# Block sums from VectorE to GpSimd, more result buffers, and four row blocks by way of HBM, in a two-layer float32 decoder trunk

## The chip, the cores and the metric

The kernel runs on one core of a Trainium2 chip. The core has five engines that each take their instructions in order: PE (TensorE: matrix products and transposes, weights loaded beside them as PEld), DVE (VectorE), ACT (ScalarE), POOL (GpSimd) and SP (SyncE, which here only issues DMAs). They work beside each other and wait for each other by semaphores. The metric is the time of one execution on the device, in microseconds (us), lower is better.

## The reference, cut to what matters

A trunk of two layers over 1024 tokens of 1024 features, all in float32. Layer 0 mixes tokens by latent attention (MLA), layer 1 by a gated linear recurrence (HGRN2); each is followed by a squared-ReLU MLP with 4096 hidden features. Every part stands between two RMS norms and adds to the residual stream.

```
def sq_relu_mlp(h, w1, w2):
    a = jax.nn.relu(h @ w1)
    return (a * a) @ w2

for layer in range(DEPTH):
    a = rms_norm(h, norm_gains[layer, 0])
    m = mla_mixer(a, ...) if layer % 2 == 0 else hgrn2_mixer(a, ...)
    h = h + rms_norm(m, norm_gains[layer, 1])
    a = rms_norm(h, norm_gains[layer, 2])
    h = h + rms_norm(sq_relu_mlp(a, mlp_w1[layer], mlp_w2[layer]), norm_gains[layer, 3])
```

## The kernel before

A float32 product is made of three products of halves: `split` writes a rounded high part (ACT, L75) and the rest (DVE, L76), and `mm3` (L80 to L82) multiplies high by high, high by low and low by high. Most of ACT's and DVE's work is such splits of weights (tile `w`) that SP has loaded into a `raw` tile. There are two `raw` tiles beside each other and five `w` tiles in turn.

The stages in the trace are MLA with its output projection (to about 500 us), the first MLP's up-projection (to 840) and down-projection (to 1165), HGRN2 (to 1735), and the second MLP's up- (to 2110) and down-projection (to the end). Both MLP projections use a seven-product block scheme after Strassen: sums of blocks are formed first, seven products take the place of eight, and results are added up.

*Up-projection*, `mlp_up`. The activations lie transposed as four blocks (`A` and `whole`). `tsums` (L736 to L742 hold half of its eight sums for each of two k) makes four further blocks T1 to T4 from them, 128x1024 values each time. The weights come in 16 blocks p. For the first eight (EARLY) a first loop makes the products that need no T; ACT copies and squares these into `h` tiles (L771, L772; L780 for the copy), which go to HBM (`psp`, `hsp`). Then a second loop runs `others` for all p: four weight-block sums of 128x512 (L793, L794, L796, L797) into `s` tiles, their splits, five products, nine additions of results (L801 to L833), and seven results to HBM from POOL's queue (`spill`, L768). For early p, SP loads back the two results. The `h` tiles are a ring of 10 (layer 0) or 8 (layer 1), the `s` tiles of 3.

*Down-projection*, `mlp_down`. In two halves c, and in each the seven products i = 0, 1, 4, 2, 5, 6, 3 with four block pairs q: the left factor is loaded from `hsp` (`raw`, `sx`), the right is a weight block or a sum of two (t1 to t4, less22; L921, L930, L935, L939, L996; 128x1024). `gather` adds up results (L982). In the second half of the first MLP the rows are finished on the way (`finish_rows`: mean square on ACT, power on POOL, L196 and L197 on DVE, a store to `res` from SP, L198, and the norm for the next part, L201). `into_features` transposes such a row block on PE (L174) and splits it into `A`.

*HGRN2.* Sixteen steps (token half, head), with projections by `featproj` (sigmoid of f on ACT, L1094), an elementwise part and `core_products`. The first eight steps use the first four row blocks of `A` (tokens 0 to 511), the last eight the other four.

A scheduler decides the order of the instructions on each engine from the program's order and priorities; `LAG` holds offsets by which transposes are put later. SP's loads of one kind keep the program's order.

## Time and profile before

| | |
|---|---|
| three timed runs | 2417.41, 2423.98, 2420.9 us; median 2420.9 |
| profiled execution | 2420.12 us |
| its span, first to last instruction | 2418.4 us |
| granted TensorE clock, mean | 0.980 |
| instructions | 30758 |

The profile is a page with busy shares by engine and groups of instructions, and a trace that can be asked for each engine's waits, for windows and for a timeline. In a group's row stand line, engine, operation, output<-inputs, shape and count, then busy us, mean ns of one, and the engine's idle time just before such instructions with what ended it. In the timeline a row holds start, duration, engine, line and operation, and in brackets the idle time before it. PEclk is the granted clock of TensorE as a share of full speed. Where the time goes is shown with the prediction.

### The profile page before, as it was taken

To read this page: it belongs to the slowest core of one execution; us is meant where nothing else is said; L and a number is where in the kernel's file an instruction comes from. 1 tells how busy PE (TensorE), PEld (TensorE's weight loads), DVE (VectorE), ACT (ScalarE), POOL (GpSimd) and SP (SyncE) were. 2 spreads that over 40 slices of the span, in tenths; PEclk is the share of its full clock that TensorE was granted. 3 is DMA by queue.
4 is the path that set the end of the run, shared out by engine and by line. 5 is a ranking of instruction groups with operands and counts; after the bars stand their busy time and mean duration, and the time that the engine had idled before them with its cause. 6 is when DMAs were issued, how large, how long until landed. Compare 5 with 4: busy or idle time off the path is not lost. (4 is left out here: it accounts for less than half of the span.)

```text
span 2418.4 us, 30758 instructions
## 1 busy us (share of the span) xinstructions
PE 2292.8 (95%) x11487; PEld 1926.0 (80%) x11487; DVE 1615.8 (67%) x2311; ACT 1178.3 (49%) x1910; POOL 343.2 (14%) x686
## 2 busy tenths in 40 slices
PE   9999999978999999999899999999888999999988
PEld 8889998757788778877688888888666778888876
DVE  5658884575766566578765667756776766576578
ACT  5445554453444444434656556665453445443433
POOL 1300000111211200001232213321211212100002
PEclk9999999989999999999899999999999999999999
DMA  6100002565554574544612224222455544664644
GB/s 214 31 22 10 10 10 92 200 198 166 202 174 144 176 284 141 183 174 140 200 53 88 77 89 126 84 70 85 142 178 196 180 161 141 219 250 131 232 143 164
DMA packets 228388, 337.32 MB, mean 139 GB/s; under 512 B 16871, under 2 KB 136718, under 8 KB 228238
## 3 DMA queue, kind: packets, MB, share of 16 engines
q1 hardware_dynamic: 209038, 272.42, 34.8%
q0 software_dynamic: 19200, 62.93, 7.0%
q8 instruction: 90, 1.47, 0.3%
q14 instruction: 60, 0.49, 0.1%
HBM read 253.51 MB, written 81.79 MB: 139 GB/s over the span
## 5 line engine op out<-in xcount | busy, mean ns | idle before, releaser
L76 DVE TENSOR_TENSOR w<-raw,w 128x1024 fp32r<-128x1024 f32 (+1 forms) x256 | 279.0, 1094 | 193.8 <-ACT w L75 192.9
L75 ACT ACTIVATE w<-raw 128x1024 fp32r<-128x1024 f32 (+1 forms) x256 | 241.6, 948 | 228.5 <-PE mm L82 122.4
L80 PE MATMUL mm<-A,w 128*128 128x512 f32 x832 | 330.7, 398 | 15.5 <-ACT h L771 11.0
L75 ACT ACTIVATE w<-s 128x1024 fp32r<-128x1024 f32 x156 | 165.2, 1060 | 347.4 <-PE c L82 124.7
L81 PE MATMUL mm<-A,w 128*128 128x512 f32 x832 | 329.0, 395 | 1.0 <-DVE A L76 1.0
L82 PE MATMUL mm<-A,w 128*128 128x512 f32 x832 | 326.6, 393 | 0.0
L76 DVE TENSOR_TENSOR w<-s,w 128x1024 fp32r<-128x1024 f32 x156 | 190.5, 1222 | 113.3 <-ACT w L75 113.1
L143 POOL TENSOR_TENSOR rstd<-rstd,nhalf 128x1 f32<-128x1 f32 x56 | 61.8, 1105 | 1056.9 <-DVE rstd L142 963.2
L80 PEld LDWEIGHTS mm<-A,w 128*128 128x128 f32 x832 | 158.1, 190 | 55.6 <-ACT h L771 16.1
L768 POOL DMA_DIRECT2D hsp<-h x224 | 121.2, 542 | 479.0 <-ACT h L772 229.0
L82 PEld LDWEIGHTS mm<-A,w 128*128 128x128 f32 x832 | 158.4, 190 | 33.2
L81 PEld LDWEIGHTS mm<-A,w 128*128 128x128 f32 x832 | 158.4, 190 | 32.8 <-DVE A L76 1.4
L81 PE MATMUL mm<-w,w 128*128 128x512 f32 x432 | 171.3, 397 | 10.6 <-DVE w L76 10.5
L82 PE MATMUL mm<-w,w 128*128 128x512 f32 x432 | 169.7, 394 | 0.0
L80 PE MATMUL mm<-w,w 128*128 128x512 f32 x432 | 155.2, 394 | 12.4 <-ACT w L75 6.5
L80 PE MATMUL mm<-w,A 128*128 128x256 f32 (+2 forms) x384 | 120.7, 316 | 3.3 <-ACT A L75 3.1
L82 PE MATMUL mm<-w,A 128*128 128x256 f32 (+2 forms) x384 | 120.3, 315 | 0.0
L81 PE MATMUL mm<-w,A 128*128 128x256 f32 (+2 forms) x384 | 119.3, 312 | 0.0
L771 ACT ACTIVATE h<-h 128x512 f32<-128x512 f32 x96 | 60.0, 625 | 106.4 <-DVE h L812 69.8
L80 PEld LDWEIGHTS mm<-w,w 128*128 128x128 f32 x432 | 81.9, 190 | 32.3 <-ACT w L75 9.5
L81 PEld LDWEIGHTS mm<-w,w 128*128 128x128 f32 x432 | 82.2, 190 | 31.7 <-DVE w L76 14.8
L82 PE MATMUL c<-T,w 128*128 128x512 f32 x256 | 98.7, 389 | 1.2 <-DVE w L76 1.2
(394 smaller groups left out, 5671.3 us busy)
## 6 DMA issues: line engine op xcount, KB each, us to landing
hsp<-h POOLq DMA_DIRECT2D x224, 256.0 KB, 3.0
raw<-in_mlp_w_dram SPq DMA_DIRECT2D x108, 512.0 KB, 3.9
s<-in_mlp_w_dram SPq DMA_DIRECT2D x80, 512.0 KB, 7.2
raw<-hsp SPq DMA_DIRECT2D x76, 512.0 KB, 4.0
raw<-in_hgrn_w_in_dram SPq DMA_DIRECT2D x64, 512.0 KB, 4.1
sx<-hsp SPq DMA_DIRECT2D x36, 512.0 KB, 4.0
res<-xt SPq DMA_DIRECT2D x24, 512.0 KB, 3.7
xt<-res SPq DMA_DIRECT2D x22, 512.0 KB, 4.5
```

The lines of the kernel that those rows point to most:

```text
L75: ACT.activation(dst[:, 0], src, AF.Copy)
L76: DVE.tensor_tensor(dst[:, 1], src, dst[:, 0].bitcast(F32), ALU.subtract)
L80: PE.matmul(ps, lhs[0], rhs[0], start=start, stop=False, skip_group_check=more)
L81: PE.matmul(ps, lhs[0], rhs[1], start=False, stop=False, skip_group_check=more)
L82: PE.matmul(ps, lhs[1], rhs[0], start=False, stop=stop, skip_group_check=more)
L143: POOL.tensor_tensor(r, r, nhalf[:, :1], ALU.pow)
L768: POOL.dma_start(hsp[i, p * P:(p + 1) * P, :], h)
L771: ACT.activation(h, src, AF.Relu)
```

## The change

1. The four weight-block sums in `others` go from DVE to POOL, in both layers (128 instructions), as do four of the eight T sums for each k (a and e: 16 instructions) and the five kinds of block sum in `mlp_down` (80 instructions).
2. The tile `whole` gets a pool of its own that is closed after `tsums`; in its place come further result buffers `h2` (4 in layer 0, 8 in layer 1), used by every odd call of `h512`.
3. `finish_rows` issues its store from POOL's queue instead of SP's. Its input tile can be loaded ahead (`rows_in`, into `s11` tiles); the last down-projection uses the same.
4. At the end of the first MLP the row blocks 4 to 7 are no longer transposed: POOL stores them in HBM (`later`), and in steps 2 to 5 of HGRN2 SP loads one each into a raw tile, where it is transposed and split into `A`.
5. `LAG` loses an entry, and its third is 250 instead of 150.

```diff
@@ -35,7 +35,7 @@
 ROPE_BASE = 10000.0
-LAG = (150, 100, 150, 300)
+LAG = (150, 100, 250)
 EARLY = 8
@@ -88,6 +88,7 @@
     ysp = new(dram, [S, D // 2], F32, "ysp")
+    later = new(dram, [S // 2, D], F32, "later")
@@ -185,17 +186,18 @@
-    def finish_rows(wp, y, ms, gpost, gpre, src, dst, t, xt_bufs=2):
+    def finish_rows(wp, y, ms, gpost, gpre, src, dst, t, xt_bufs=2, xt=None):
         rows = slice(t * P, (t + 1) * P)
-        xt = new(wp, [P, D], F32, "xt", xt_bufs)
-        tc.keep_in_program_order(SP.dma_start(xt, src[rows, :]))
+        if xt is None:
+            xt = new(wp, [P, D], F32, "xt", xt_bufs)
+            tc.keep_in_program_order(SP.dma_start(xt, src[rows, :]))
         if ms is None:
...
         DVE.scalar_tensor_tensor(xt, y, r, xt, ALU.mult, ALU.add)
-        SP.dma_start(dst[rows, :], xt)
+        POOL.dma_start(dst[rows, :], xt)
         if gpre is not None:
@@ -650,7 +652,8 @@
-            A["whole"] = new(p, [P, 4, KT // 2, P], F32, "whole")
+            act["whole"] = ExitStack()
+            A["whole"] = new(pool(act["whole"], "whole", side="right"), [P, 4, KT // 2, P], F32, "whole")
@@ -733,13 +736,13 @@
                     split(T2[:, :, k:k + 2], d)
-                    DVE.tensor_tensor(by_tile(a), by_tile(part(B22, 0)), b12, ALU.subtract)
-                    DVE.tensor_tensor(a, a, part(B22, 1), ALU.add)
+                    POOL.tensor_tensor(by_tile(a), by_tile(part(B22, 0)), b12, ALU.subtract)
+                    POOL.tensor_tensor(a, a, part(B22, 1), ALU.add)
                     split(T1[:, :, k:k + 2], b)
...
                     e = d
-                    DVE.tensor_tensor(e, part(B21, 0), d, ALU.subtract)
-                    DVE.tensor_tensor(e, e, part(B21, 1), ALU.add)
+                    POOL.tensor_tensor(e, part(B21, 0), d, ALU.subtract)
+                    POOL.tensor_tensor(e, e, part(B21, 1), ALU.add)
                     split(T4[:, :, k:k + 2], e)
@@ -747,7 +750,12 @@
+            hs = {"n": 0, "more": None}
+
             def h512():
+                hs["n"] += 1
+                if hs["more"] and hs["n"] % 2:
+                    return new(hs["more"], [P, 512], F32, "h2", 4 if layer == 0 else 8)
                 return new(wp, [P, 512], F32, "h", 10 if layer == 0 else 8)
@@ -790,11 +798,11 @@
                 s34 = new(wp, [P, 1024], F32, "s", 3).rearrange("p (k c) -> p k c", c=256)
-                DVE.tensor_tensor(s12[:, :, :P], rA[:, :, P:], rB[:, :, P:], ALU.add)
-                DVE.tensor_tensor(s12[:, :, P:], s12[:, :, :P], rA[:, :, :P], ALU.subtract)
+                POOL.tensor_tensor(s12[:, :, :P], rA[:, :, P:], rB[:, :, P:], ALU.add)
+                POOL.tensor_tensor(s12[:, :, P:], s12[:, :, :P], rA[:, :, :P], ALU.subtract)
                 wS12 = w_parts(s12)
-                DVE.tensor_tensor(s34[:, :, :P], rA[:, :, :P], rA[:, :, P:], ALU.subtract)
-                DVE.tensor_tensor(s34[:, :, P:], rB[:, :, :P], s12[:, :, P:], ALU.subtract)
+                POOL.tensor_tensor(s34[:, :, :P], rA[:, :, :P], rA[:, :, P:], ALU.subtract)
+                POOL.tensor_tensor(s34[:, :, P:], rB[:, :, :P], s12[:, :, P:], ALU.subtract)
                 b = new(PG, [P, 512], F32, "tr")
@@ -840,6 +848,9 @@
             tsums()
+
+            act["whole"].close()
+            hs["more"] = pool(act["stack"], f"more{layer}", side="right")
             for p in range(NP):
@@ -918,7 +929,7 @@
                     load11(q)
-                    DVE.tensor_tensor(s11[q], b12, s11[q], ALU.subtract)
+                    POOL.tensor_tensor(s11[q], b12, s11[q], ALU.subtract)
                     return s11[q]
@@ -927,16 +938,16 @@
                     t = new(wr, [P, 2, 512], F32, "s12", 3)
-                    DVE.tensor_tensor(t, s22[q], s11[q], ALU.subtract)
+                    POOL.tensor_tensor(t, s22[q], s11[q], ALU.subtract)
                     return t
...
                     b12 = load12(q)
-                    DVE.tensor_tensor(b12, s22[q], b12, ALU.subtract)
+                    POOL.tensor_tensor(b12, s22[q], b12, ALU.subtract)
                     return b12
...
                 def t4(q):
-                    DVE.tensor_tensor(s21[q], s21[q], s11[q], ALU.add)
+                    POOL.tensor_tensor(s21[q], s21[q], s11[q], ALU.add)
                     return s21[q]
@@ -957,9 +968,11 @@
-                def by_tiles(i, banks, right, n1, done, own_tile):
+                def by_tiles(i, banks, right, n1, done, own_tile, then=None):
                     fs = [factors(i, q, right, own_tile) for q in qs[n1:]]
+                    if then is not None:
+                        then()
                     for tt in range(4):
@@ -993,7 +1006,7 @@
                 def less22(q):
-                    DVE.tensor_tensor(s21[q], s21[q], s22[q], ALU.subtract)
+                    POOL.tensor_tensor(s21[q], s21[q], s22[q], ALU.subtract)
@@ -1011,6 +1024,12 @@
                 gather(c22, Y, c22)
+                def rows_in(t):
+
+                    xt = new(wp, [P, 2, 512], F32, "s11", KC // 2).rearrange("p a b -> p (a b)")
+                    tc.keep_in_program_order(SP.dma_start(xt, src[t * P:(t + 1) * P, :]))
+                    return xt
+
                 if not last:
@@ -1024,17 +1043,14 @@
                         DVE.tensor_tensor(c21[t], Y[t], U[t], ALU.add)
-                        finish_rows(wp, y[4 + t], None, gpost, gpre, src, dst, 4 + t)
-                        with tc.high_priority(offset=-LAG[3]):
-                            into_features(y[4 + t], act["A"], 4 + t)
+                        finish_rows(wp, y[4 + t], None, gpost, gpre, src, dst, 4 + t, xt=xts[t])
+                        POOL.dma_start(later[t * P:(t + 1) * P, :], y[4 + t])
                     product(3, Y, t4, True, n1=2)
-                    by_tiles(3, Y, t4, 2, done, False)
+                    xts = []
+                    by_tiles(3, Y, t4, 2, done, False, lambda: xts.extend(rows_in(4 + t) for t in range(4)))
                 else:
-                    xts, s22s, yg = {}, {}, {}
-                    for t in range(4, NT):
-                        xts[t] = new(wp, [P, D], F32, "xf", 2) if t < 6 else new(wp, [P, D], F32, "xt", 2)
-                        SP.dma_start(xts[t], src[t * P:(t + 1) * P, :])
+                    s22s, xts = {}, []
                     for t in range(4):
@@ -1042,7 +1058,7 @@
                         rows = slice((4 + t) * P, (5 + t) * P)
-                        xt = xts[4 + t]
+                        xt = xts[t]
                         DVE.tensor_tensor(c21[t], Y[t], U[t], ALU.add)
@@ -1052,7 +1068,7 @@
-                    by_tiles(3, Y, t4, 0, done, True)
+                    by_tiles(3, Y, t4, 0, done, True, lambda: xts.extend(rows_in(4 + t) for t in range(4)))
                     sr.close()
@@ -1275,6 +1291,11 @@
                 proj_v(half, h // 2)
+            if 1 < si < 6:
+
+                r = raw_tile()
+                SP.dma_start(r, later[(si - 2) * P:(si - 1) * P, :])
+                into_features(r, A, si + 2)
             with tc.high_priority(offset=100):
@@ -1286,7 +1307,8 @@
                 gpre = row_bcast(wp, "gpre", norm_gains[1, 2], D)
-                acc = new(pool(act["stack"], "acc", side="right"), [P, 4, D], F32, "acc")
+                act["whole"] = ExitStack()
+                acc = new(pool(act["whole"], "acc", side="right"), [P, 4, D], F32, "acc")
```

Three places show how the instructions stand.

At the end of the first MLP, on PE: `mm` here are HGRN2's projections, `tr` the transposed rows y4 to y7. Before:

```order
L82 MATMUL mm_1607_10020<-w_1604_9966,A10_1511_9503 128x256
L174 MATMUL tr_1541_9678<-ident_5_64,y4_1227_7509 128x128 x4
L174 MATMUL tr_1542_9685<-ident_5_64,y4_1227_7509 128x128 x4
L174 MATMUL tr_1551_9725<-ident_5_64,y5_1228_7510 128x128 x4
L174 MATMUL tr_1552_9732<-ident_5_64,y5_1228_7510 128x128 x4
L174 MATMUL tr_1561_9772<-ident_5_64,y6_1229_7511 128x128 x4
L174 MATMUL tr_1562_9779<-ident_5_64,y6_1229_7511 128x128 x4
L174 MATMUL tr_1571_9819<-ident_5_64,y7_1230_7512 128x128 x4
L174 MATMUL tr_1572_9826<-ident_5_64,y7_1230_7512 128x128 x4
L80 MATMUL mm_1618_10120<-A00_1509_9501,w_1617_10117 128x512
```

At the same place after:

```order
L80 MATMUL mm_1600_9977<-w_1597_9923,A10_1512_9512 128x256
L81 MATMUL mm_1600_9977<-w_1597_9923,A10_1512_9512 128x256
L82 MATMUL mm_1600_9977<-w_1597_9923,A10_1512_9512 128x256
L80 MATMUL mm_1611_10077<-A00_1510_9510,w_1610_10074 128x512
L81 MATMUL mm_1611_10077<-A00_1510_9510,w_1610_10074 128x512
L82 MATMUL mm_1611_10077<-A00_1510_9510,w_1610_10074 128x512
```

The eight groups of four transposes are gone; the next projection (`mm`, with `A00`) follows the last one at once.

In the last half of the second layer's down-projection, on DVE (`s11`, `s12`, `s21`, `s22`: weight blocks and their sums; `w`: their splits). Before:

```order
L76 TENSOR_TENSOR w_2988_18748<-raw_2987_18746,w_2988_18748 128x1024
L76 TENSOR_TENSOR w_2991_18756<-s11_2990_18753,w_2991_18756 128x1024
L76 TENSOR_TENSOR w_2993_18785<-sx_2992_18783,w_2993_18785 128x1024
L996 TENSOR_TENSOR s21_2959_18533<-s21_2959_18533,s22_2999_18829 128x1024
L930 TENSOR_TENSOR s12_3019_18977<-s22_2999_18829,s11_2980_18679 128x1024
L939 TENSOR_TENSOR s21_2959_18533<-s21_2959_18533,s11_2980_18679 128x1024
L996 TENSOR_TENSOR s21_2963_18567<-s21_2963_18567,s22_3003_18864 128x1024
L930 TENSOR_TENSOR s12_3023_19011<-s22_3003_18864,s11_2985_18716 128x1024
L76 TENSOR_TENSOR w_2996_18793<-s11_2995_18790,w_2996_18793 128x1024
L76 TENSOR_TENSOR w_2998_18826<-raw_2997_18824,w_2998_18826 128x1024
```

After, DVE:

```order
L76 TENSOR_TENSOR w_2991_18744<-s11_2990_18741,w_2991_18744 128x1024
L76 TENSOR_TENSOR w_2993_18773<-raw_2992_18771,w_2993_18773 128x1024
L76 TENSOR_TENSOR w_2996_18781<-s11_2995_18778,w_2996_18781 128x1024
L76 TENSOR_TENSOR w_2998_18810<-sx_2997_18808,w_2998_18810 128x1024
L76 TENSOR_TENSOR w_3001_18818<-s11_3000_18815,w_3001_18818 128x1024
L76 TENSOR_TENSOR w_3003_18851<-raw_3002_18849,w_3003_18851 128x1024
L76 TENSOR_TENSOR w_3005_18856<-s22_3004_18854,w_3005_18856 128x1024
L76 TENSOR_TENSOR w_3007_18886<-raw_3006_18884,w_3007_18886 128x1024
```

And the sums of that place, now on POOL:

```order
L1009 TENSOR_TENSOR s21_2964_18558<-s21_2964_18558,s22_3004_18854 128x1024
L941 TENSOR_TENSOR s12_3024_19002<-s22_3004_18854,s11_2985_18704 128x1024
L1009 TENSOR_TENSOR s21_2968_18592<-s21_2968_18592,s22_3008_18889 128x1024
L941 TENSOR_TENSOR s12_3028_19036<-s22_3008_18889,s11_2990_18741 128x1024
L950 TENSOR_TENSOR s21_2964_18558<-s21_2964_18558,s11_2985_18704 128x1024
L1009 TENSOR_TENSOR s21_2972_18626<-s21_2972_18626,s22_3012_18924 128x1024
L941 TENSOR_TENSOR s12_3032_19070<-s22_3012_18924,s11_2995_18778 128x1024
L950 TENSOR_TENSOR s21_2968_18592<-s21_2968_18592,s11_2990_18741 128x1024
```

The splits stand one behind the other on DVE; the sums that stood between them are in POOL's order, among themselves.

In the first layer's `tsums`, on DVE (`s`: sums, `T1` to `T3`: their splits, `w`: a split of the early loop). Before:

```order
L731 TENSOR_TENSOR s_910_5408<-s_910_5408,A00_745_4340 128x1024
L733 TENSOR_TENSOR s_911_5409<-A11_747_4342,s_910_5408 128x1024
L736 TENSOR_TENSOR s_909_5407<-A11_747_4342,whole_748_4343 128x1024
L76 TENSOR_TENSOR T1_852_5070<-s_910_5408,T1_852_5070 128x1024
L734 TENSOR_TENSOR s_911_5409<-s_911_5409,A11_747_4342 128x1024
L737 TENSOR_TENSOR s_909_5407<-s_909_5407,A11_747_4342 128x1024
L730 TENSOR_TENSOR s_913_5427<-whole_748_4343,A00_745_4340 128x1024
L76 TENSOR_TENSOR w_879_5220<-raw_875_5199,w_879_5220 128x512
L76 TENSOR_TENSOR T2_849_5067<-s_911_5409,T2_849_5067 128x1024
L731 TENSOR_TENSOR s_913_5427<-s_913_5427,A00_745_4340 128x1024
L76 TENSOR_TENSOR T3_850_5068<-s_909_5407,T3_850_5068 128x1024
```

After, on POOL, whose stores of the early loop (`psp`, `hsp`) stand around the sums:

```order
L847 DMA psp_849_5067<-h_858_5095 128x512
L739 TENSOR_TENSOR s_910_5411<-A11_748_4343,whole_749_4347 128x1024
L740 TENSOR_TENSOR s_910_5411<-s_910_5411,A11_748_4343 128x1024
L847 DMA psp_849_5067<-h_865_5137 128x512
L776 DMA hsp_848_5066<-h_860_5113 128x512
L744 TENSOR_TENSOR s_912_5413<-A10_747_4342,s_912_5413 128x1024
L745 TENSOR_TENSOR s_912_5413<-s_912_5413,A10_747_4342 128x1024
```

And on ACT, where the split into `T3` reads POOL's sum `s_910`:

```order
L75 ACTIVATE T1_853_5074<-s_911_5412 128x1024
L779 ACTIVATE h_860_5113<-mm_857_5082 128x512
L788 ACTIVATE h_865_5137<-mm_864_5124 128x512
L75 ACTIVATE w_880_5224<-raw_876_5203 128x512
L75 ACTIVATE T2_850_5071<-s_912_5413 128x1024
L780 ACTIVATE h_860_5113<-h_860_5113 128x512
L75 ACTIVATE T3_851_5072<-s_910_5411 128x1024
L75 ACTIVATE T1_853_5074<-s_914_5431 128x1024
L75 ACTIVATE w_887_5266<-raw_883_5245 128x512
L779 ACTIVATE h_867_5155<-mm_864_5124 128x512
L788 ACTIVATE h_872_5179<-mm_871_5166 128x512
```

The two sums for T3 (L736 and L737 before) stand on POOL now, and ACT's T3 split still stands ahead of the next Relu and copy of early results (L779, L788).

## The prediction

> **What bounds the kernel now.** I read the page's busy shares first, then TensorE's waits, then windows around the widest waits, then the timeline of the engine each wait names.
>
> ```profile
> PE 2292.8 (95%) x11487; PEld 1926.0 (80%) x11487; DVE 1615.8 (67%) x2311; ACT 1178.3 (49%) x1910; POOL 343.2 (14%) x686
> ```
>
> TensorE (PE) is busy for 95% of the 2418.4 us span; VectorE (DVE) for 67%, GpSimd (POOL) for 14%. The matmuls are the same in number after the change, so all it can win is in the 5% in which PE stands still or runs at a lower clock. Taking time off DVE wins nothing by itself; it wins where PE waits for DVE. TensorE's waits, by what released them:
>
> ```profile
> PE mm L80 <- ACT h L771: 11.0, 12, 3.3
> PE tr L80 <- DVE h L801: 10.6, 2, 7.5
> PE mm L81 <- DVE w L76: 10.5, 8, 4.4
> PE tr L174 <- DVE acc L201: 9.5, 2, 5.1
> PE tr L174 <- DVE A L76: 8.9, 3, 4.2
> PE tr L82 <- DVE w L76: 6.0, 6, 1.6
> PE mm L80 <- DVE y L982: 5.9, 3, 3.8
> ```
>
> (The columns: who waits, for whom, total us, times, longest.) Five of these seven rows the change can reach: L771 and L801 (up-projection), w L76 on L81 and y L982 (down-projection), and A L76 (end of the first MLP). The acc row is the end of hgrn, where PE's order stays and the chain of products, norm and transposes is the same: nothing there. Of the tr L82 row I count nothing.
>
> **Why DVE is late.** Engines take instructions in order. DVE's own groups show what holds it:
>
> ```profile
> L793 DVE TENSOR_TENSOR s<-raw,raw 128x512 f32<-128x512 f32 x32 | 22.1, 691 | 47.0 <-DMA raw<-in_mlp_w_dram 47.0
> L935 DVE TENSOR_TENSOR s<-s,s 128x1024 f32<-128x1024 f32 x16 | 19.6, 1225 | 17.4 <-DMA s<-in_mlp_w_dram 17.3
> L921 DVE TENSOR_TENSOR s<-s,s 128x1024 f32<-128x1024 f32 x16 | 19.5, 1221 | 15.1 <-DMA s<-in_mlp_w_dram 15.1
> L996 DVE TENSOR_TENSOR s<-s,s 128x1024 f32<-128x1024 f32 x16 | 19.5, 1220 | 11.9 <-DMA s<-in_mlp_w_dram 11.9
> ```
>
> The last number is DVE's idle time in front of the group: 47.0 + 17.4 + 15.1 + 11.9 = 91 us in which a block sum at the head of DVE's queue waits for a load, and whatever stands behind it waits too. All four groups go to POOL. One such place, in the second layer's down-projection, DVE's timeline (start, duration), then PE's:
>
> ```profile
> 2302.60 1.23 DVE L996 TENSOR_TENSOR s<-s,s 128x1024 f32<-128x1024 f32 x1 [5.26 <-DMA s<-in_mlp_w_dram]
> 2303.74 1.22 DVE L930 TENSOR_TENSOR s<-s,s 128x1024 f32<-128x1024 f32 x1
> 2304.88 1.22 DVE L939 TENSOR_TENSOR s<-s,s 128x1024 f32<-128x1024 f32 x1
> 2306.01 1.22 DVE L996 TENSOR_TENSOR s<-s,s 128x1024 f32<-128x1024 f32 x1
> 2307.15 1.22 DVE L930 TENSOR_TENSOR s<-s,s 128x1024 f32<-128x1024 f32 x1
> 2308.28 1.22 DVE L76 TENSOR_TENSOR w<-s,w 128x1024 fp32r<-128x1024 f32 x1
> ...
> 2309.56 0.79 PE L81 MATMUL mm<-w,w 128*128 128x512 f32 x1 [4.38 <-DVE w L76]
> ```
>
> DVE sits 5.26 us on a load, does five sums (5.7 us), and only then the weight split that PE stood 4.38 us for. After the change the split has no sum before it.
>
> **The change, part by part.** The sum is made against the profiled execution, 2420.1 us (span 2418.4 and 1.7 us around it); the three timed runs have median 2420.9, so the two are taken as one.
>
> *Amount moved.* Off DVE: 128 sums of 128x512 at 0.69 us (88 us) and 96 of 128x1024 at 1.22 us (117 us): 205 us, 13% of its busy time. That is no gain yet. What they cost on POOL, by the rows nearest:
>
> ```profile
> L1145 POOL TENSOR_TENSOR e<-f 128x512 f32<-128x512 f32 x16 | 17.4, 1087 | 0.0
> L463 POOL TENSOR_TENSOR qrt<-ra,rb 128x256 f32<-128x256 f32 x8 | 6.0, 746 | 13.3 <-DVE rb L461 13.2
> L768 POOL DMA_DIRECT2D hsp<-h x224 | 121.2, 542 | 479.0 <-ACT h L772 229.0 <-DVE h L823 166.5 <-DVE h L826 34.1
> ```
>
> A 128x512 sum takes 1.09 us (L1145, same shape), at most 1.49 (twice L463); a 128x1024 sum, which no row shows, 2.2 us (twice L1145), at most 3.0. POOL gains 128 x 1.09 + 96 x 2.2 = 350 us on 343: far from full over the span.
>
> *Down-projection (80 sums).* Per pair of blocks PE works 24 matmuls; at the pace between these two starts, 0.23 us, that is 5.5 us.
>
> ```profile
> 2316.13 0.40 PE L82 MATMUL c<-w,w 128*128 128x512 f32 x1
> 2316.36 0.40 PE L80 MATMUL c<-w,w 128*128 128x512 f32 x1
> ```
>
> DVE keeps two splits (2.44 us), POOL has one sum (2.2 us); even one after the other, 4.7 us fit in 5.5. In passes with two sums per pair they need not (6.8), as two on DVE did (4.9); those sums are wanted a pass later, so they can spread. PE's waits here are 10.5 + 5.9 = 16.4 us, and behind each PE resumes at a lower clock: in the window from 2300 PEclk is 0.83, so 3.4 of 20 us, of which the waits themselves are part. I put the whole at 22 us and take half, **-11** (0 to -22): half, because a sum that waits for a late load is still waited for, on POOL, by the product that needs it.
>
> ```profile
> 1180.00:1200.00 20.00, 11.13 (x66) 9.74 (x66) 16.14 (x20) 10.24 (x19) 6.53 (x17) 0.73 0.77 234
> 1200.00:1220.00 20.00, 16.66 (x76) 13.37 (x75) 12.19 (x15) 15.96 (x21) 7.82 (x18) 0.76 0.09 33
> 2300.00:2320.00 20.00, 13.50 (x46) 10.28 (x45) 17.40 (x17) 6.57 (x7) 0.00 (x0) 0.83 0.36 124
> ```
>
> (Window; length; busy us and instructions of PE, weight load, DVE, ACT, POOL; PEclk; DMA share; GB/s.)
>
> *End of the first MLP.* PE has the transposes of y4 to y7 in its order, each behind ACT's and DVE's finishing of that row:
>
> ```profile
> 1189.59 1.97 PE L174 MATMUL tr<-ident,y 128*128 128x128 f32 x8 [3.21 <-DVE A L76]
> 1195.75 1.97 PE L174 MATMUL tr<-ident,y 128*128 128x128 f32 x8 [4.19 <-DVE A L76]
> 1199.19 1.97 PE L174 MATMUL tr<-ident,y 128*128 128x128 f32 x8 [1.48 <-DVE A L76]
> 1202.90 0.80 PE L80 MATMUL mm<-A,w 128*128 128x512 f32 x1 [1.74 <-ACT f L1094]
> ```
>
> The three waits are 8.9 us, at clocks 0.73 and 0.76. They go. What is late next is ACT's first sigmoid (L1094): ACT still takes the mean squares of y4 to y7 first, and PE's products of the first head wait for what follows. That chain also runs through DVE, where the 8 splits of A go from between the rows:
>
> ```profile
> L76 DVE TENSOR_TENSOR A<-tr,A 128x512 fp32r<-128x512 f32 x40 | 26.6, 684 | 3.3 <-ACT A L75 3.3
> ```
>
> It ends about 8 x 0.68 = 5.5 us sooner, and PE's head start beyond that is lost in waiting for the sigmoid. The transposes return in hgrn at full clock: four rows at 1.97 x 0.73 = 1.4 us, 5.8 us of PE as against 7.9 here. The four stores and four loads of `later` lie on POOL's and SP's queues, 512 KB each, two hgrn steps ahead of their use. I take **-6** (0 to -14, the waits and the clock's share).
>
> *Up-projection behind the T sums.* Reachable waits: 10.6 (L801) + 11.0 (L771) - 3.3 (the longest, inside the early phase) = 18 us. L793's 47 us at the head of DVE's queue go to POOL's, where the spills (0.54 us each, 7 per p) queue behind them instead; the extra `h2` buffers take up that delay. Half again: **-9** (0 to -18).
>
> *T sums (16 sums).* POOL's four per k now feed ACT's T3 and T4 splits, and ACT's next Relu, whose result frees PE's PSUM bank, is behind them. How POOL fares beside a busy DVE, three rows of two places (and "..." between them):
>
> ```profile
> 1120.79 6.09 POOL L143 TENSOR_TENSOR rstd<-rstd,nhalf 128x1 f32<-128x1 f32 x1 [276.65 <-DVE rstd L142]
> ...
> 1209.65 1.52 POOL L1145 TENSOR_TENSOR e<-f 128x512 f32<-128x512 f32 x1
> 1210.18 1.53 DVE L1143 TENSOR_TENSOR kr<-kr,kk 128x512 f32<-128x512 f32 x1
> ```
>
> An operation on one column took 6.09 us while DVE ran two-input instructions back to back; and L1145 and L1143 lengthened each other to 1.5 us, where DVE's other 128x512 sums take 0.69. So a POOL sum and a DVE sum with both inputs in SBUF run one after the other, and POOL can starve. The Trainium skill says so ("SBUF — State Buffer", section "SBUF: two separate sides": the port pair that both engines use is held for a whole instruction), and these rows agree; by its rule POOL's 1024-wide sum would also hold each DVE split for up to 2.2 us. Not every DVE instruction excludes: here the DVE pair reads PSUM, and the POOL sum beside it keeps its 0.74 us.
>
> ```profile
> 119.69 1.27 DVE L166 SCALAR_TENSOR_TENSOR q<-mm,q 128x512 fp32r<-128x512 f32 x2
> 119.85 0.74 POOL L463 TENSOR_TENSOR qrt<-ra,rb 128x256 f32<-128x256 f32 x1 [2.02 <-DVE rb L461]
> ```
>
> Before the T3 split DVE has about eight instructions in a row, 9 us; POOL's two sums then take 4.4. Against the old order (two DVE sums, 2.4 us) T3 is up to 7 us later, in each layer. DVE has 4 x 1.22 = 4.9 us less per k, which gives some back. **+4** for both layers (-3 to +14).
>
> *Late raw tiles.* A raw tile is free when its last sum is done: up to 4 x (1.09 - 0.69) = 1.6 us later in 16 early p's, and the loads of L801's input queue on SP behind raw loads. Mostly hidden, because POOL reaches its sums sooner than DVE did: **+3** (0 to +16).
>
> *Stores of finished rows* go from SP's queue to POOL's: SP no longer waits for L197 ahead of raw loads. Its use is inside the terms above; without it nothing.
>
> Sum: -11 - 6 - 9 + 4 + 3 = -19: 2420.1 - 19 = **2401 us**.
>
> **The rivals.**
>
> *POOL becomes the late one (slower).* In an early p PE works 60 matmuls x 0.23 = 13.8 us. DVE keeps 9 sums of h (6.2 us) and splits of 1.22 + 1.22 + 0.69 = 3.1 us: 9.3. POOL's four sums are 4.4 us. If every DVE instruction excluded POOL, 13.7 of 13.8 us would be taken; this decides from 1.1 us per sum, exactly where L1145 stands. If only those with two SBUF inputs exclude (3.1 + 4 x 0.69 = 5.9 us), there is room for 2.0 us per sum; L463 beside L166 speaks for this. In the first case T sums cost 14, the early p's 16, the up-projection gains nothing, the down-projection keeps 5 of its gain and the end of the first MLP 6: 2420 + 30 - 11 = 2439 us. The Trainium skill's rule ("GPSIMD Engine Reference", section 4.1, an elementwise add belongs on VectorE, about twice as fast) speaks for this rival; L1145's 1.09 against 0.69 us agrees with its direction.
>
> *Loads, not DVE, are late (no change).* The same L793 row says the load came late; if a product waits for the load anyway, the two middle terms fall away: -6 + 3 = 2417 us. Against it: at 2308.28 the split did not need the load that DVE's queue stood on.
>
> *All reachable waits go.* -22 - 14 - 18 + 4 = -50: 2370 us. Against it: L771 has 12 waits of about a microsecond, the mark of a steady limit.
>
> **How the numbers follow.** Chances: forecast 0.50, all waits go 0.14, no change 0.13, slower 0.23. A measurement here can tell 0.3% (7.3 us) from nothing: faster is 0.50 + 0.14 = 0.64, same 0.13, slower 0.23. The range runs from 2372, by the third rival, to 2436, by the first: it leaves out half of each, under 2 in 10.
>
> **What would show it.** Right: the waits for w L76 and y L982 in the down-projections at half of 16 us; no PE transposes near 1190 to 1200 and PEclk there above 0.9; DVE's idle time on weight loads gone. Wrong: PE waits of 5 us and more for ACT's h in the early phase, near 520 and 1780; POOL sums of 1.5 us and more; PE's wait for L801's successor growing. A gain in hgrn itself would be outside this account.

## The result and the profile after

| | before | after |
|---|---|---|
| median, us | 2421.14 (4 runs, 2417.41 to 2423.98) | 2485.76 (4 runs, 2482.53 to 2489.35) |
| ratio | | 1.0268, 95% interval 1.0247 to 1.0289 |
| span of the profiled execution, us | 2418.4 | 2482.4 |
| mean granted clock | 0.980 | 0.971 |

The change made the kernel slower by 64.6 us; 2401 was forecast, with a range up to 2436. The page's busy times after:

```profile
PE 2309.8 (93%) x11487; PEld 1934.3 (78%) x11487; DVE 1642.0 (66%) x2087; ACT 1169.2 (47%) x1905; POOL 831.9 (34%) x942
```

DVE has 224 instructions fewer, 205 us of work at the old durations, and is busy for 26 us *more*: what stayed on it has become 231 us longer. POOL gained 489 us, not 350. The groups of DVE's weight splits and of POOL's sums show where (columns as before: count, busy us, mean ns, idle before). The first row is of the kernel before, the others of the changed kernel:

```profile
L76 DVE TENSOR_TENSOR w<-s,w 128x1024 fp32r<-128x1024 f32 x156 | 190.5, 1222 | 113.3 <-ACT w L75 113.1
...
L76 DVE TENSOR_TENSOR w<-s,w 128x1024 fp32r<-128x1024 f32 x156 | 250.6, 1608 | 150.2 <-ACT w L75 149.9
L76 DVE TENSOR_TENSOR w<-sx,w 128x1024 fp32r<-128x1024 f32 x40 | 61.9, 1548 | 10.1 <-ACT w L75 10.0
L941 POOL TENSOR_TENSOR s<-s,s 128x1024 f32<-128x1024 f32 x16 | 53.7, 3358 | 13.6 <-DVE w L76 13.6
L932 POOL TENSOR_TENSOR s<-s,s 128x1024 f32<-128x1024 f32 x16 | 47.8, 2995 | 212.2 <-DMA s<-in_mlp_w_dram 212.2
L804 POOL TENSOR_TENSOR s<-raw 128x512 f32<-128x512 f32 x32 | 50.3, 1571 | 11.2 <-DVE w L76 11.1
```

A split of 128x1024 took 1.22 us before and 1.6 on average now, though not one is changed. POOL's sums take 2.5 to 3.4 us at 128x1024 (means of their groups), where 2.2 was assumed, and 1.4 to 1.6 at 128x512, where 1.09 was. What reads PSUM is not longer: L816, a sum of results with one source in PSUM, takes 0.69 us as before, while L841, with both sources in SBUF, went from 0.69 to 1.01. DVE's waits for weight loads did go (POOL's L932 now stands on them for 212 us), as the prediction said, but DVE now waits longer for ACT's high parts, 381 us against 317, and what went was worth less than the lengthening. Four of PE's widest waits:

```profile
PE mm L80 <- ACT h L779: 37.0, 12, 9.0
PE mm L81 <- DVE w L76: 20.9, 14, 4.2
PE mm L80 <- DVE h L816: 20.6, 8, 5.2
PE mm L80 <- ACT f L1110: 7.6, 1, 7.6
```

L779 is the old L771, the Relu of the early loop: 11.0 us before, 37.0 now. DVE's w on L81, of which half was to go, has doubled. Two signs by which the prediction was to be known as wrong are here: PE's waits of over 5 us for ACT's h in the early loops (6.2 us near 520, 9.0 near 1820), and POOL's sums of over 1.5 us. The third did not come: PE's wait for L801's successor, L809, is gone.

**A table by stage.** Starts of stages can't be compared, because the scheduler lets matmuls of one stage run within the next. So I worked out, from each trace, the *lost time*: for each pair of PE instructions the time from start to start less the undisturbed pace of that width (0.227 us for 512 columns, 0.119 for 256, 0.11 for 128), summed by stage. It holds waits and lower clocks alike. It misses none of the difference: 185.3 us before and 248.6 after are 63.3 apart, the spans 64.0. Stages are the early loop with the T sums, the rest of the up-projection behind it, the down-projection (each for layers 0 and 1), the end of the first MLP up to hgrn's first core product, and hgrn. MLA and the end of hgrn, 30 to 33 and 17 to 18 us in each kernel, are in the total alone. The columns other than the first two are the experiments below.

| lost time, us | before | after | u_tsums | u_others | u_down | no_sums | t_dummy | no_h2 | buf_store | u_later | buf_only | others_pool | less_pool |
|---|---|---|---|---|---|---|---|---|---|---|---|---|---|
| early loop 0 | 13.1 | 30.0 | 14.2 | 28.6 | 28.7 | 12.2 | 26.1 | 12.2 | 13.2 | 30.3 | 13.3 | 14.5 | 13.5 |
| behind it 0 | 20.4 | 21.2 | 20.3 | 20.6 | 23.6 | 17.6 | 19.3 | 21.0 | 18.5 | 20.3 | 18.4 | 20.0 | 19.9 |
| down 0 | 19.6 | 20.1 | 16.0 | 18.0 | 14.7 | 11.0 | 14.5 | 18.5 | 13.2 | 21.6 | 14.2 | 13.6 | 19.8 |
| end of MLP 0 | 17.2 | 20.1 | 19.5 | 19.6 | 19.8 | 18.2 | 18.5 | 18.5 | 17.4 | 16.3 | 14.4 | 18.1 | 16.9 |
| hgrn | 22.7 | 30.7 | 28.8 | 28.6 | 31.7 | 32.6 | 30.8 | 31.2 | 20.8 | 18.6 | 19.5 | 21.3 | 21.6 |
| early loop 1 | 8.4 | 26.9 | 9.2 | 25.7 | 24.7 | 9.0 | 8.6 | 8.7 | 8.5 | 23.9 | 8.5 | 9.3 | 8.9 |
| behind it 1 | 20.7 | 20.5 | 18.5 | 20.8 | 13.5 | 13.9 | 12.6 | 20.7 | 14.3 | 16.8 | 15.3 | 19.8 | 16.4 |
| down 1 | 16.3 | 29.8 | 29.6 | 30.0 | 14.9 | 15.7 | 15.0 | 15.5 | 18.2 | 28.5 | 14.5 | 15.3 | 22.2 |
| total | 185.3 | 248.6 | 204.3 | 243.1 | 221.2 | 178.8 | 195.6 | 197.0 | 172.5 | 225.0 | 167.3 | 180.5 | 188.9 |

Of the 63 us, 35 come in the two early loops, 14 in the down-projections (13.5 of them in layer 1), 8 in hgrn and 3 at the end of the first MLP. Each column is one execution, and some rows move by 7 to 8 us where the edit touches nothing: u_down leaves the second up-projection as it is, and the stretch behind its early loop goes from 20.5 to 13.5; no_h2 leaves the down-projections, and the first goes from 11.0 to 18.5 against no_sums. The cause of that is not known. So a difference of up to 8 us in one row is not safely the edit's own; those of 12 us and more, on which the main readings rest, are larger.

**The early loop, first layer.** Rows of POOL's timeline, then DVE's and ACT's, then PE's waits there, all of the changed kernel (start, duration; brackets: idle before):

```profile
503.68 2.38 POOL L739 TENSOR_TENSOR s<-A,whole 128x1024 f32<-128x1024 f32 x1
506.14 3.25 POOL L740 TENSOR_TENSOR s<-s,A 128x1024 f32<-128x1024 f32 x1
...
516.95 3.25 POOL L744 TENSOR_TENSOR s<-A,s 128x1024 f32<-128x1024 f32 x1 [1.76 <-DVE T L76]
...
504.06 3.09 DVE L734 TENSOR_TENSOR s<-s,A 128x1024 f32<-128x1024 f32 x1
507.19 3.28 DVE L736 TENSOR_TENSOR s<-A,s 128x1024 f32<-128x1024 f32 x1
510.39 1.21 DVE L76 TENSOR_TENSOR T<-s,T 128x1024 fp32r<-128x1024 f32 x1
...
507.19 1.06 ACT L75 ACTIVATE T<-s 128x1024 fp32r<-128x1024 f32 x1 [3.92 <-DVE s L734]
512.77 1.06 ACT L75 ACTIVATE T<-s 128x1024 fp32r<-128x1024 f32 x1 [3.04 <-DVE s L737]
519.60 0.63 ACT L75 ACTIVATE w<-raw 128x512 fp32r<-128x512 f32 x1 [3.36 <-DMA raw<-in_mlp_w_dram]
520.14 0.58 ACT L779 ACTIVATE h<-mm 128x512 f32<-128x512 f32 x1
...
508.78 0.50 PE L80 MATMUL mm<-A,w 128*128 128x512 f32 x1 [1.04 <-ACT h L779]
520.77 0.79 PE L80 MATMUL mm<-A,w 128*128 128x512 f32 x1 [6.23 <-ACT h L779]
530.18 0.50 PE L80 MATMUL mm<-A,w 128*128 128x512 f32 x1 [2.18 <-ACT h L779]
```

The two DVE sums that stand beside POOL's take 3.1 and 3.3 us; the split at 510.39, when POOL is done, takes 1.21 again. ACT, in order, waits for DVE's lengthened sums, and the Relu that PE waits for (L779) stands behind ACT's waits. There is a second way from DVE to PE: the widest wait shown, 6.23 us, ends with a Relu that stood behind a split for which ACT waited 3.36 us on a weight load. That load came late because DVE freed its raw tile late: SP issued a load at 515.76 us, when DVE's split at 515.05 had just ended. Between 498 and 575 us SP's queue waits 38.9 us for DVE's splits; before the change it waits 1.6 us there for DVE. ACT's waits on weight loads in the loop (500 to 562 us) are 19.3 us, against 8.2 before. POOL does not starve: its first sum runs beside DVE in 2.38 us, and of its 128x1024 sums in the whole kernel none took over 3.4. It is DVE that is held.

### The profile page after: what moved, and what is told of

Same layout as the page of the kernel before. It is cut to its first block, busy times and chain, and to the rows that moved or that the text cites. A ratio compares the mean times of both kernels' runs of the same rounds, so it can differ in the third digit from the quotient of the medians.

```text
span 2482.4 us, 30905 instructions
## 1 busy us (share of the span) xinstructions
PE 2309.8 (93%) x11487; PEld 1934.3 (78%) x11487; DVE 1642.0 (66%) x2087; ACT 1169.2 (47%) x1905; POOL 831.9 (34%) x942
## 5 line engine op out<-in xcount | busy, mean ns | idle before, releaser
L76 DVE TENSOR_TENSOR w<-raw,w 128x1024 fp32r<-128x1024 f32 (+1 forms) x256 | 360.4, 1414 | 222.5 <-ACT w L75 221.4
L80 PE MATMUL mm<-A,w 128*128 128x512 f32 x832 | 339.1, 409 | 67.6 <-ACT h L779 37.0
L76 DVE TENSOR_TENSOR w<-s,w 128x1024 fp32r<-128x1024 f32 x156 | 250.6, 1608 | 150.2 <-ACT w L75 149.9
L81 PE MATMUL mm<-A,w 128*128 128x512 f32 x832 | 336.6, 405 | 1.0 <-DVE A L76 1.0
L82 PE MATMUL mm<-A,w 128*128 128x512 f32 x832 | 334.2, 403 | 0.5 <-DVE w L76 0.5
L80 PEld LDWEIGHTS mm<-A,w 128*128 128x128 f32 x832 | 162.7, 196 | 111.7 <-ACT h L779 42.0
L81 PE MATMUL mm<-w,w 128*128 128x512 f32 x432 | 173.1, 401 | 20.5 <-DVE w L76 20.5
L82 PEld LDWEIGHTS mm<-A,w 128*128 128x128 f32 x832 | 162.8, 196 | 35.7 <-DVE w L76 1.1
L81 PEld LDWEIGHTS mm<-A,w 128*128 128x128 f32 x832 | 162.8, 196 | 34.2 <-DVE A L76 1.5
L81 PE MATMUL mm<-w,A 128*128 128x256 f32 (+2 forms) x384 | 119.0, 311 | 0.4 <-DVE w L76 0.4
L932 POOL TENSOR_TENSOR s<-s,s 128x1024 f32<-128x1024 f32 x16 | 47.8, 2995 | 212.2 <-DMA s<-in_mlp_w_dram 212.2
L81 PEld LDWEIGHTS mm<-w,w 128*128 128x128 f32 x432 | 82.9, 192 | 43.4 <-DVE w L76 26.4
L779 ACT ACTIVATE h<-h 128x512 f32<-128x512 f32 x96 | 60.1, 626 | 111.5 <-DVE h L820 85.0
```

The source lines that it names most:

```text
L76: DVE.tensor_tensor(dst[:, 1], src, dst[:, 0].bitcast(F32), ALU.subtract)
L80: PE.matmul(ps, lhs[0], rhs[0], start=start, stop=False, skip_group_check=more)
L81: PE.matmul(ps, lhs[0], rhs[1], start=False, stop=False, skip_group_check=more)
L82: PE.matmul(ps, lhs[1], rhs[0], start=False, stop=stop, skip_group_check=more)
L779: ACT.activation(h, src, AF.Relu)
L932: POOL.tensor_tensor(s11[q], b12, s11[q], ALU.subtract)
```

## The experiments

**One group of sums back at a time, then all three.** Each kernel is the changed one with `POOL.` back to `DVE.` in these lines:

```diff
# u_tsums: L739, L740, L744, L745     u_others: L801, L802, L804, L805
# u_down:  L932, L941, L946, L950, L1009     no_sums: all thirteen
-                    POOL.tensor_tensor(a, a, part(B22, 1), ALU.add)
+                    DVE.tensor_tensor(a, a, part(B22, 1), ALU.add)
```

> The changed kernel with the 16 T sums back on DVE. Theory 1 (a GpSimd sum and a DVE instruction with two SBUF inputs exclude each other, and in the early loops the T sums stand in the chain that frees PE's PSUM banks): the two early loops, 16.9 and 18.5 us longer than before the change, come back to within 4 us of before; about 2486 - 31 = 2455 us. Theory 2 (the early loops are slow because the new buffers put a load of results between SP's raw loads): the early loops stay at least 12 us longer than before each, 2475 us or more.

Measured 2440.32 us (1.0084, 1.0063 to 1.0104). The early loops lose 14.2 and 9.2 us, within about 1 us of before the change: theory 1. The gain of 45 us is larger than expected because later stages are quieter too.

> The changed kernel with the 128 weight-block sums of the up-projection back on DVE. Theory 1: the stretches behind the early loops (6.2 and 8.0 us longer than before) come back and may beat before, by the extra buffers: 2486 - 14 = 2472 us, to 2465. Theory 2: they stay, since not the sums but the loads' order is late there; 2480 us or more.

2477.7 us (1.023, 1.0204 to 1.0255), between the two; and the stretches behind the early loops do not move (21.2 to 20.6, 20.5 to 20.8). The 6.2 and 8.0 us in this expectation were differences of starting times of stages, which hold different numbers of matmuls. By lost time there was nothing to come back. Within these stretches one wait does follow the sums, that of PE for DVE's L816: 1.5 us before (L808), 20.6 in the changed kernel, and 17.5 to 19.8 in u_tsums, u_down, u_later and others_pool, which all have these sums on POOL; with them on DVE 3.2 here and 2.2 in no_sums. What it costs in the changed kernel other waits make up for here: PE's wait for L809, gone there, is back with 5.3 us.

> The changed kernel with the 80 down-projection sums back on DVE. In the first layer this stage became 5.0 us shorter with the change, in the second 5.4 us longer. Theory 1: the sums on GpSimd won the head-of-queue waits and lost as much by exclusion, so undoing them changes little: 2480 to 2492 us, the first layer's stage 5 us longer, the second's 5 us shorter. Theory 2 (the second layer's loss is from rows loaded ahead for the end, not from sums): the second layer's stage stays long and the whole is 2490 us.

2460.32 us (1.0163, 1.0143 to 1.0183). Both theories missed, by the same misreading: the sums on POOL cost 5.4 us in the first layer and 14.9 in the second, and in neither is anything won. The place in the changed kernel's second layer, DVE's and POOL's timelines and the PE instruction that waited:

```profile
2370.69 3.35 POOL L941 TENSOR_TENSOR s<-s,s 128x1024 f32<-128x1024 f32 x1
2374.01 6.72 POOL L950 TENSOR_TENSOR s<-s,s 128x1024 f32<-128x1024 f32 x2
2380.70 3.32 POOL L1009 TENSOR_TENSOR s<-s,s 128x1024 f32<-128x1024 f32 x1
2384.10 3.23 POOL L950 TENSOR_TENSOR s<-s,s 128x1024 f32<-128x1024 f32 x1
...
2375.05 3.42 DVE L76 TENSOR_TENSOR w<-sx,w 128x1024 fp32r<-128x1024 f32 x1
2378.51 3.31 DVE L76 TENSOR_TENSOR wx<-s,wx 128x1024 fp32r<-128x1024 f32 x1
2381.74 3.36 DVE L76 TENSOR_TENSOR w<-s,w 128x1024 fp32r<-128x1024 f32 x1
2385.03 3.38 DVE L76 TENSOR_TENSOR w<-raw,w 128x1024 fp32r<-128x1024 f32 x1
2385.16 0.79 PE L81 MATMUL mm<-w,w 128*128 128x512 f32 x1 [4.22 <-DVE w L76]
```

POOL's five sums in a row and DVE's splits take turns, one of each in 3.3 us. Two splits per block pair are then 6.7 us, and PE works 5.5 on a pair. A run of sums on POOL slows *every* split beside it here, not only the split that needs a sum.

> The changed kernel with all three groups of sums back on DVE; what stays is the extra result buffers, the rows by way of HBM and the stores from GpSimd's queue. Theory 1: nearly all of the loss was the sums: 2425 us, of which 11 us are the hgrn stage (the transposed rows now lie in it) and some is won by the buffers; at most 2435. Theory 2: the loss is in buffers and loads' order: 2455 us or more.

2416.58 us (0.9985, 0.9972 to 0.9999): theory 1, and a little better than expected. With all sums back nearly the whole loss is gone, and what stays of the change is worth 3 us in sum.

**Exclusion alone, without a wait for the result.** no_sums, and in the first layer's T sums:

```diff
+                    if layer == 0:
+                        g = new(wp, [P, 1024], F32, "g", 1).rearrange("p (k c) -> p k c", c=512)
...
+                    if layer == 0:
+                        for i in range(4):
+                            POOL.tensor_tensor(g, part(B22, i % 2), part(B11, i % 2), ALU.add)
```

> The kernel of the run before (all sums on DVE, 2416.6 us), and beside it eight further sums of 128x1024 on GpSimd in the first layer's T sums alone, at the place where the change has its own; nobody uses their result, and nothing is left out. Theory 1a (exclusion alone: a GpSimd sum holds up DVE's splits): the first layer's early loop grows by 8 us or more of the 16, the second layer's by nothing; 2425 us or more. Theory 1b (ACT's queue, which waits for GpSimd's result ahead of the Relu that frees PE's bank): under 3 us; 2417 to 2419 us.

2431.97 us (1.0041, 1.0028 to 1.0054). The first layer's early loop loses 26.1 us (12.2 without these sums), the second's 8.6: theory 1a. Its timeline, POOL, then DVE and ACT:

```profile
504.34 9.02 POOL L751 TENSOR_TENSOR g<-A,A 128x1024 f32<-128x1024 f32 x3
...
504.72 3.09 DVE L736 TENSOR_TENSOR s<-s,A 128x1024 f32<-128x1024 f32 x1
507.84 3.27 DVE L738 TENSOR_TENSOR s<-A,s 128x1024 f32<-128x1024 f32 x1
511.03 3.41 DVE L741 TENSOR_TENSOR s<-A,whole 128x1024 f32<-128x1024 f32 x1
521.20 2.19 ACT L75 ACTIVATE T<-s 128x1024 fp32r<-128x1024 f32 x2 [10.29 <-DVE s L739]
```

Nobody waits for `g`, and still ACT waits 10.29 us for DVE. Exclusion alone is thus enough for 13.9 us; the changed kernel loses 17.8 here beyond no_sums. The one is not a part of the other: here DVE keeps all its eight sums for each two k beside POOL's four, there it has four. How much a wait for POOL's result adds is not told apart.

**The price by itself.** A kernel of nothing but sums, 12 in each stretch. Between stretches stands a gate: three sums, on DVE, POOL and DVE, each of which needs the one before it.

```diff
+    for i in range(N):
+        DVE.tensor_tensor(u, u, a, ALU.add)
+        POOL.tensor_tensor(v, v, a, ALU.add)
+    gate()
```

> Not the trunk: only sums on two engines are done, 12 of each kind in each stretch, and the outputs are not the reference's. Theory 1: DVE alone 1.22 us and GpSimd alone 2.4 us at 128x1024; beside each other with both inputs in SBUF, each pair takes 3.6 us (the sum of both), so both read about 3.6 us. With one of DVE's inputs in PSUM both keep their time. Rival (they share bandwidth): beside each other 1.5 to 2 times longer each, and a pair shorter than the sum.

Its groups: DVE alone (L107), POOL alone (L110), both at 128x1024 (L113, L114), POOL with a DVE that reads PSUM and SBUF (L123, and L121, half of DVE's sums there), and POOL with a DVE operation of one SBUF input (L129, L130):

```profile
L107 DVE TENSOR_TENSOR u<-u,b 128x1024 f32<-128x1024 f32 x12 | 14.7, 1226 | 0.4
L110 POOL TENSOR_TENSOR v<-v,b 128x1024 f32<-128x1024 f32 x12 | 28.1, 2339 | 2.2 <-DVE u L101 1.3
L113 DVE TENSOR_TENSOR u<-u,a 128x1024 f32<-128x1024 f32 x12 | 36.9, 3076 | 0.4
L114 POOL TENSOR_TENSOR v<-v,a 128x1024 f32<-128x1024 f32 x12 | 38.6, 3215 | 2.2 <-DVE u L101 1.3
L121 DVE TENSOR_TENSOR u<-pt,a 128x512 f32<-128x512 f32 x12 | 8.2, 682 | 0.0
L123 POOL TENSOR_TENSOR v<-v,b 128x1024 f32<-128x1024 f32 x12 | 28.1, 2346 | 2.2 <-DVE u L101 1.3
L129 DVE TENSOR_SCALAR u<-a 128x1024 f32<-128x1024 f32 x12 | 30.5, 2542 | 0.4
L130 POOL TENSOR_TENSOR v<-v,a 128x1024 f32<-128x1024 f32 x12 | 32.2, 2682 | 2.2 <-DVE u L101 1.3
```

Alone 1.23 and 2.34 us, 3.57 together; beside each other 12 pairs take 39.4 us, 3.3 a pair. That is nine tenths of the sum of both: one after the other with little overlap, a little less than theory 1's 3.6. The rival does not fit: DVE's sum is 2.5 times as long, POOL's 1.4 times. With PSUM as one of DVE's sources neither is longer: POOL's sum takes 2.35 us, and DVE's, three of which run within one of POOL's, 0.68, against 0.69 for its 128x512 sums of either kind in the kernel before. The pairs are the 3.2 to 3.4 us of the kernel.

**The other parts.** no_h2 is no_sums with `if False:` in `h512`; buf_store is no_sums with the transposes at the end of the first MLP as before, and with `LAG`'s third entry, an offset for the rows that hgrn finishes, at its old 150:

```diff
-LAG = (150, 100, 250)
+LAG = (150, 100, 150)
...
-                        POOL.dma_start(later[t * P:(t + 1) * P, :], y[4 + t])
+                        with tc.high_priority(offset=-300):
+                            into_features(y[4 + t], act["A"], 4 + t)
...
-            if 1 < si < 6:
+            if False:
```

> All sums on DVE and every result in the old ring of buffers; rows by way of HBM and stores from GpSimd's queue stay. If the extra buffers made the second layer's stretch behind the early loop 5.9 us shorter, it is lost: 2420 to 2424 us. If not they but the stores' queue did it: 2414 to 2418 us.

2436.7 us (1.0061, 1.0048 to 1.0074), well above the range expected: the extra buffers are worth 18 us in lost time (197.0 against 178.8), 7.5 in the first down-projection, 6.8 behind the second layer's early loop and 3.4 behind the first's. The kernel's own times agree, 20 us apart. Why the first down-projection, which uses none of these buffers, should gain is open.

> All sums on DVE, and the rows 4 to 7 transposed at the end of the first MLP again (the old offset too); the extra buffers, the rows loaded ahead and the stores from GpSimd's queue stay. If the rows by way of HBM only move the time from the end of the MLP (12 us shorter) into hgrn (12.6 us longer): 2413 to 2420 us. If hgrn's extra time has another cause: 2425 us or more, since the 12 us at the end of the MLP are lost.

2409.25 us (0.9947, 0.9934 to 0.9959), better than expected: the way by HBM does not only move time, it costs. hgrn loses 20.8 us in place of 32.6, and the end of the MLP 17.4 in place of 18.2, so it gained nothing there. The offset in `LAG` changed with it and was not tried by itself, but it acts where a half's rows are finished, from the ninth step on, and the difference lies before: from the first core product to the eighth's, PE loses 14.5 us in no_sums and 2.7 in buf_store, and behind that nearly the same in both. What SP waits for around hgrn's first steps, in the changed kernel from 1205 to 1405, and in buf_store from 1205 to 1400:

```profile
SPq L631 <- PE tr L175: 62.2, 4, 29.3
SPq L631 <- DVE w L76: 50.4, 13, 22.8
...
SPq L631 <- DVE w L76: 178.8, 27, 23.7
```

L631 loads hgrn's weights. The four rows lie in raw tiles until PE transposes them, up to 29.3 us, and the weight loads that need the tile wait on SP's queue; without `later` there is no such wait, though SP then waits longer for DVE's splits. It is doubtful that PE is late by this: from the first core product on, its own waits in these steps name DVE's elementwise work above all and no split of weights. In no_sums they are 4.0 us for `qq`, 2.2 for `kT` and 2.5 for others, in buf_store 2.6 in all. By what step the way by HBM costs these 12 us stays open.

> The changed kernel (all three groups of sums on GpSimd) with the rows 4 to 7 transposed at the end of the first MLP again, and the old offset. If the way by HBM costs the 11.8 us of PE loss in hgrn that the run before last showed between two kernels without sums, here too: 2486 - 8 to 12 = 2474 to 2478 us, hgrn's loss back from 30.7 to 21 us. If it pays where GpSimd is loaded (the end of the MLP is then later): 2482 us or more.

2459.82 us (1.0152, 1.0137 to 1.0168): 26 us less than the changed kernel, a larger gain than expected. hgrn's loss is back at 18.6, 12 us less as between the two kernels without sums, the end of the MLP at 16.3, and 3 to 4 us each go in the second layer's up-projection, which the edit does not touch. Why the way by HBM costs 24 us of lost time beside the sums and 6 without them stays open.

> All sums on DVE, rows not by way of HBM, finished rows stored from SP's queue as before: what stays of the change are the extra buffers and the rows loaded ahead. The kernel with the stores on GpSimd's queue took 2409.3 us. If the stores' queue matters little (24 stores, SP waiting for L197 ahead of raw loads): 2407 to 2412 us. If it is worth its own, 2415 us or more.

The edit to buf_store is `SP.dma_start` in place of `POOL.dma_start` for the finished rows. 2400.93 us (0.9912, 0.9899 to 0.9925): the fastest of all, 21 us below before, and below both ranges. The stores on POOL's queue cost 8 us (5 in the lost time of the two traces: end of the MLP 17.4 to 14.4, second down-projection 18.2 to 14.5). What waits behind them was not settled.

> The kernel of 2409.3 us with the 128 weight-block sums of the up-projection alone on GpSimd. Theory 1 with a point from which it decides: a pair of a GpSimd sum and a DVE instruction takes nearly the sum of both, so these sums cost 4 x 1.26 = 5 us of a DVE that is free 4.5 of 13.8 us in an early p (7.9 counting the ones that read PSUM as free): little or nothing is lost there, and nothing won; 2406 to 2415 us. If the sums alone are worth the half of the up-projection's waits that the prediction gave them: 2400 us.

2416.71 us (0.9973, 0.9962 to 0.9984): 7 us above the kernel without them and just outside the range; the second layer loses 19.8 in place of 14.3 us behind the early loop. Nothing of the forecast half of the waits is won: PE's waits for L809 (2.3 us in buf_store) go, and those for L816 grow from 1.9 to 19.8 us.

> The kernel of 2409.3 us with only the sums less22 (16 of the 80 of the down-projection) on GpSimd: the ones at which DVE's queue stood on a load at the place that the prediction quoted. If taking a waiting head out of DVE's queue pays where few splits stand beside it: 2402 to 2406 us. If the exclusion eats it there as well: 2409 to 2418 us.

2423.63 us (1.0001, 0.9989 to 1.0013), 14 us above its base: 16 sums alone, on the very place that the prediction showed, cost 6.6 us in the first and 4.0 in the second down-projection by lost time, each within what untouched rows move by; the 14 us of the whole are not. Three in a row at 2300.42 take 9.97 us of POOL, 3.3 each, beside DVE's splits and the sums that stayed.

## Why the prediction was wrong

*The starting point* held: PE bounds, DVE's queue stood on loads, and moving the sums took that away. *What replaced it* was in the prediction, in part, as the first rival's mechanism, with a chance of 0.23 and too low a price: the rival gave 2439, the kernel took 2486. It was also not that rival as written. The rival let every DVE instruction exclude POOL and put 16 us of its loss on the early p's of the up-projection, with 5 us still won in the down-projection; in the runs those that read PSUM do not exclude, the up-projection behind the T sums lost 0.6, and the down-projection lost 14.

*The step that failed* is the sum for the down-projection, which took the exclusion to be harmless there. The prediction wrote that a POOL sum "would also hold each DVE split for up to 2.2 us", added two splits and one sum to 4.7 us per block pair (2.44 + 2.2 is 4.6), and found that "even one after the other" they "fit in 5.5"; for two sums per pair it had 6.8 us and took it that these "can spread". They do not spread: POOL has several sums at hand when loads land, five in a row in the place shown, and then each split has one beside it, 2 x 3.3 = 6.7 us per pair. The term was -11 (0 to -22) and measured +14: not half the waits gone, but more of them.

*The T sums* were +4 with a bound of +14; they measured +35 in the two early loops. This is the largest miss of the sum. The bound came from POOL starving behind nine microseconds of DVE, read from a power on one column that took 6.09 us. The runs showed the reverse for the sums: POOL takes its turn at once, each DVE sum beside it goes from 1.22 us to between 3.1 and 3.4, and ACT with the Relu behind it waits for DVE and for weight loads that DVE's splits release late. t_dummy shows this without any use of POOL's result.

*Up-projection behind them*, -9, and late raw tiles, +3: measured +0.6 together. This hides two things: the buffers win 10 us there (no_h2 against no_sums), and the sums on POOL give much of it back (others_pool, 5.5 and 1.5 us against buf_store, and PE's new waits for L816). That the second is the sums of this stage alone is not shown, since u_others takes them back and finds nothing. The waits for L801 that were to be halved did go, but the gain there is the buffers', to which the prediction gave no price of their own: without them PE waits 10.8 us for that instruction (L809 in no_h2), with them 2.2 (no_sums).

*End of the first MLP*, -6: measured +3, and +8 in hgrn. The prediction named what is late next, the first sigmoid, and PE now waits 7.6 us for it (L1110) in one piece. That hgrn itself would lose by the rows' way through HBM, 12 us in both pairs of kernels that differ in it and in the `LAG` entry, it did not count; by what step stays open. *Stores*, "inside the terms above": 8 us, in the wrong direction. In the second rival, whose 2417 us is -6 + 3, the +4 of the T sums is left out without a reason; with it the rival gives 2421, and nothing else rests on it.

*The price of a sum*: 2.2 us was near (2.34 alone in ports), and 1.09 at 128x512 a little low (1.26 alone); what was mis-sized is less the sum than the company it keeps. The Trainium skill ("SBUF — State Buffer", section "SBUF: two separate sides") says that the loser of the shared port pair waits for the whole instruction; the runs nearly agree, 3.3 us a pair against 3.57 for the sum of both.

## What to carry to other kernels

GpSimd is no second VectorE beside a VectorE that works from SBUF: add both durations for every such pair (3.3 us here, 3.57 by the sum), at the worst moment and not on average, before moving elementwise work to it. DVE's work with one source in PSUM was free of that here. Part a change before judging it: here 21 us of gain (more result buffers and rows loaded ahead) lay under 85 us of loss.

## What was not expected of the hardware

One DVE operation with a single SBUF input, and none in PSUM, excludes GpSimd as well: `tensor_scalar` at 128x1024 took 2.54 us beside POOL's sum, where the kernel before has 0.75 for one of that shape (L562, in MLA), and POOL's sum took 2.68 instead of 2.34. And in long runs of both the two engines take turns, one instruction each (five sums and five splits in the down-projection, 12 pairs in ports). It is no rule without exception: at 1820.73 us of the changed kernel a DVE split of 128x512, 0.69 us elsewhere, took 5.63 us while two POOL sums passed in 2.4 us each, as long as alone.
